# One decoder layer on one core: the compressed tokens' first layer over 129 columns, two moved steps, and a two-operation scaling on GpSimd

## The chip, the core and the metric

The kernel runs on one core of a Trainium2 chip. The metric is the device time of one execution in microseconds. Every time below comes from runs of the kernel before the change: three timed executions, and one more that was profiled.

## What is computed

One layer of a hybrid decoder for 512 tokens of width 1024, in float32. The normalised input feeds two mixers side by side: an RWKV-7 time mixing (16 heads of 64, written as chunks of 64 tokens, with a triangular inversion in each) and a sparse attention (16 heads in 4 groups, with a compressed, a selected and a sliding-window branch). Their outputs are gated, merged and projected; a gated MLP with a short convolution follows. The change touches three places of this. The compressed branch makes its keys and values so:

```
n_cmp = (S - CMP_BLOCK) // CMP_STRIDE + 1            # 31 blocks of 32 tokens, 16 apart
cidx = np.arange(n_cmp)[:, None] * CMP_STRIDE + np.arange(CMP_BLOCK)[None, :]
def compress(t, pos, w1, w2):
    blk = kv(t)[:, :, cidx] + pos.astype(f32)
    hid = jax.nn.gelu(blk.reshape(B, G, n_cmp, CMP_BLOCK * DH) @ w1.astype(f32))
    return hid @ w2.astype(f32)
```

The RWKV side shifts each projection by a token (`z = z + (prev - z) * mu`), and the attention's two softmaxes are scaled per query, each row of probabilities by one factor.

## The kernel before

Everything is one long program for TensorE, with the other four engines around it. Projections are taken in blocks of 128 output columns (`proj_steps`, L302): eight steps of three matmuls of 512 columns each (L306 to L308), since each float32 product is made of three products of split halves. These blocks are the filler: `drive` runs them as a generator, `fill`, and after each step of it lets other generators (threads, each with a delay and a rate) take a step. So a `yield` more or less in a thread moves its instructions by some steps of the filler in TensorE's order. A scheduling layer puts each engine's instructions in an order of its own from the order in which the code issues them, unless they are pinned with `keep_in_program_order`.

Compression. `cproj` (L384) makes, for keys and then for values, a tile KC of 128 partitions with 5 x 8 x 33 numbers: four groups and, as a fifth, the position part; the sixteen offsets of a pair of tokens are spread over partitions and the second index. The unused numbers are set to zero by GpSimd (L387, L390). `compress` (L405) multiplies it with the first layer's weights w1 in 16 float32 matmuls of 5 x 31 = 155 columns that add up in one PSUM bank, hid; a `yield` after every four of them puts filler between (L414). Column 124, the position part's first, becomes the bias hb (L417), which is added to the other 124 (L421). Then come a GELU and the second layer. `compress(0)` and `compress(1)` run one after the other as a thread beside the projections of pair 0.

RWKV. The 16 heads are worked on in eight pairs p, and the pairs in two groups of GP = 4. `inputs` (L493) makes K, R and V of a pair: a projection into a PSUM bank (`pj`, two banks), ScalarE's scaled copy `shift_a` (L333), then VectorE's `shift_b` (L336), which reads the bank once more and so frees it. K's `shift_b` is put in the code at the step SK = 4 of R's projection, pinned. `prep` (L526) forms the scaled vectors, ending with AR (L570) and KB; `couple` (L581) multiplies R, transposes V on TensorE (tile pv, L140 by way of `tr`), and multiplies KB with AR (tile g, L605). When a group's four pairs are done, `invert` runs a triangular inversion on VectorE as a chain of 60 instructions (tiles TM and XP, L660 and L662), while TensorE works on gate projections (gt) and, for group 0, on pair 4's K, R and V. Then the inverse is copied and transposed to TT (L674 to L683), and `recur` starts with matmuls on it (mt, L703).

Attention. For each of eight pairs of heads p8, `score` (L1051) makes the scores of both heads by blocks of 128 queries, their exponentials p with row sums (L1097, L1099), and in `norm` multiplies each tile p by its factor from stt (L1073): branch b = 0 on VectorE, b = 1 on GpSimd, 64 tiles each, of 128 to 512 columns. `values` then transposes the tiles (pt, L140), copies them out of PSUM and multiplies them with the values (o, L1146). The compressed branch's probabilities, sc, are scaled by GpSimd too (L1049) and transposed as pct. The attention of p8 = 0 starts while the last RWKV work of group 1 is finished.

Of the kernel before, what the change touches and what calls it, by code (L numbers as in the profile page):

```python
# [10 lines left out]
F32 = mybir.dt.float32  # L11
F32R = mybir.dt.float32r
AF = mybir.ActivationFunctionType
OP = mybir.AluOpType
# [9 lines left out]
NCMP = 31  # L24
# [8 lines left out]
GP = 4  # L33
# [9 lines left out]
def hybrid_layer(ctx: ExitStack, tc: tile.TileContext, a, out, dbg=None, stop=None):  # L43
# [338 lines left out]
    KCs = []  # L382

    def cproj(kv):  # L384
        KC = cp.tile([128, 5, 8, 33], F32, tag="KC", name=f"KC{kv}", bufs=2)
        KCs.append(KC)
        po.memset(KC[:, 4], 0.0)  # L387
        pos = cp.tile([64, 32], F32, tag="pos", name=f"pos{kv}", bufs=2)
        sy.dma_start(pos, a["posk" if kv == 0 else "posv"])
        po.memset(KC[:, 0:4, :, 32:33], 0.0)  # L390
        for i in range(2):
            po.tensor_copy(KC[64 * i:64 * i + 64, 4, :, 0:2].rearrange("p r q -> p q r"),
                           pos.rearrange("p (q r two) -> p q r two", r=8, two=2)[:, :, :, i])
        for half in range(2):
            p = pj(f"kc{kv}{half}")
            yield from proj_steps((35 if kv == 0 else 37) + half, f"kc{kv}{half}", p)
            z = cp.tile([128, 2, 8, 32], F32, tag="z", name=f"zc{kv}{half}", bufs=2)
            pv = p.rearrange("p (q r two) -> p two r q", r=8, two=2)
            for i in range(2):
                sc.activation(z[:, i], pv[:, i], AF.Copy)  # L400
            for e in range(2):
                for i in range(2):
                    sc.dma_start(KC[64 * i:64 * i + 64, 2 * half + e, :, 0:32], z[e * 64:e * 64 + 64, i])

    def compress(kv):  # L405
        w1 = cp.tile([128, 16, 128], F32, tag="w1", name=f"w1{kv}", bufs=2)
        sy.dma_start(w1, a["w1k" if kv == 0 else "w1v"])
        w2 = cp.tile([128, 64], F32, tag="w2", name=f"w2{kv}", bufs=2)
        sy.dma_start(w2, a["w2k" if kv == 0 else "w2v"])
        ph = pz(f"hid{kv}")  # L410
        for l in range(16):
            te.matmul(ph[:, 0:5 * NCMP], w1[:, l, :], KCs[kv][:, :, l % 8, l // 8:l // 8 + NCMP],
                      start=l == 0, stop=l == 15)
            if l % 4 == 3:  # L414
                yield
        hb = cp.tile([128, 1], F32, tag="hb", name=f"hb{kv}", bufs=2)
        ve.tensor_copy(hb, ph[:, 4 * NCMP:4 * NCMP + 1])  # L417
        u = cp.tile([128, 4, 32], F32, tag="hu", name=f"hu{kv}", bufs=2)
        w = cp.tile([128, 4, 32], F32, tag="hv", name=f"hv{kv}", bufs=2)
        po.memset(u, 0.0)  # L420
        ve.tensor_scalar(u[:, :, 0:NCMP], ph[:, 0:4 * NCMP].rearrange("p (g n) -> p g n", n=NCMP), hb, None,  # L421
                         op0=OP.add)
        ve.tensor_tensor(w, u, u, op=OP.mult)
        ve.tensor_scalar(w, w, 0.044715, 1.0, op0=OP.mult, op1=OP.add)
        ve.tensor_tensor(w, w, u, op=OP.mult)
        sc.activation(w, w, AF.Tanh, scale=float(np.sqrt(2.0 / np.pi)))
        ve.tensor_scalar(w, w, 0.5, 0.5, op0=OP.mult, op1=OP.add)
        ve.tensor_tensor(u, u, w, op=OP.mult)
        yield
        yield  # L430
        pm = pz(f"kcm{kv}")
        if kv == 0:
            te.matmul(pm[0:64, 0:128], w2, u.rearrange("p g n -> p (g n)"), start=True, stop=True)
            k4 = pm[0:64, 0:128].rearrange("p (g n) -> p g n", n=32)
            sc.activation(kcs[0:64, :, 0], k4, AF.Copy)
            ve.tensor_tensor(kcs[0:64, :, 1], k4, kcs[0:64, :, 0].bitcast(F32), op=OP.subtract)
            sy.dma_start(kcs[64:128].bitcast(F32), kcs[0:64].bitcast(F32))
        else:
            for e in range(2):
                es = slice(e * 32, e * 32 + 32)  # L440
                for g in range(4):
                    te.matmul(pm[es, g * 64:g * 64 + 64], u[:, g, :], w2, start=True, stop=True)
            for q in (0, 64):
                sc.activation(vcc[q:q + 64], pm[0:64, 0:256].rearrange("p (g d) -> p g d", d=64), AF.Copy)
# [48 lines left out]
    def inputs(p, o):  # L493
        K = o.K = rw.tile([128, S], F32, tag="K", name=f"K{p}", bufs=2)
        pk = pj(f"k{p}")
        yield from proj_steps(4 + 3 * p, f"k{p}", pk)
        shift_a(pk, K, 8 + p)
        R = o.R = rw.tile([128, S], F32, tag="R", name=f"R{p}", bufs=1)
        pr = pj(f"r{p}")
        for i, _ in enumerate(proj_steps(3 + 3 * p, f"r{p}", pr)):  # L500
            if i == SK:
                tc.keep_in_program_order(shift_b(pk, K, 8 + p))
            yield
        shift(pr, R, p)
# [76 lines left out]
    def couple(p, o, gr, i):  # L581
# [4 lines left out]
            sc.activation(AR[:, 0, :], Q, AF.Copy)  # L586
        po.tensor_tensor(AR[:, 1, :].rearrange(c8, t=64), R.rearrange(c8, t=64), EC[:, :, 1:65], op=OP.mult)
        sc.activation(gr.Dc[:, i], EC[:, :, 64], AF.Copy)
        yield
        yield  # L590
        for q in range(2):
            pv = px(f"pv{p}{q}")
            for j in range(4):
# [457 lines left out]
    def score(p8, o):  # L1051
# [11 lines left out]
        def norm(e, qb, k):  # L1063
# [6 lines left out]
                                 op=OP.mult)  # L1070
            for b in range(2):
                i = b * 4 + k
                (po if b else ve).tensor_scalar(o.pe[e, b, k], o.pe[e, b, k], st[e][:, 3, i:i + 1], None, op0=OP.mult)  # L1073

        done = []
        for e, qb in ((0, 3), (0, 2), (1, 3), (1, 2), (0, 1), (0, 0), (1, 1), (1, 0)):
# [512 lines left out]
```

## Time and profile before

| | |
|---|---|
| median of 3 runs | 1169.26 us (1168.82 to 1169.72) |
| the profiled execution's own time | 1168.92 us |
| span of that execution, first to last instruction | 1167.1 us |
| instructions in the profile | 19728 |
| busy time of DVE, ACT, POOL | 587.8, 584.0, 580.5 us |

The engines are called PE (TensorE's matmuls), PEld (its weight loads), DVE (VectorE), ACT (ScalarE), POOL (GpSimd) and SP (SyncE, which issues most DMAs). A row of the timeline has the start from the beginning of the span in us, the length in us, the engine, the line of the kernel, the operation, `out<-in` by the program's names without their numbers, the shape, the count of instructions that were merged, and in square brackets the idle time before it with what ended it. A row of the groups has the count, the busy time in us and the mean length of one in ns, then the idle time before. A float32 matmul stands as two records (64 for hid's 32), a transpose as one; starts of TensorE's records are measured, their ends are modelled, so distances between starts are the better measure.

### The profile page before, as it was taken

The page shows a single profiled execution, that of the slowest core. Times are in us where ns is not written, and L with a number is a line of the kernel's source. Part 1 is how long each engine was busy: PE and PEld are TensorE (multiplying, and loading weights), DVE is VectorE, ACT ScalarE, POOL GpSimd, SP SyncE. Part 2 cuts the span into 40 slices and gives each one's busy share as a digit, 9 for nine tenths or more (in the row PEclk, how much of TensorE's full clock was granted, in tenths as well). Part 3 has the DMA queues.
Part 4 walks back from the last instruction along what each step waited for, and adds up shares of the span by engine and source line. Part 5 has one row for each costly group of instructions (what it writes and reads, how often), then busy time and mean ns, then how long its engine had stood idle before and what let it go on. Part 6 is the DMA issues. An engine that isn't in the chain of part 4 may idle for free.

```text
span 1167.1 us, 19728 instructions
## 1 busy us (share of the span) xinstructions
PE 1145.0 (98%) x7338; PEld 916.2 (79%) x7338; DVE 587.8 (50%) x1194; ACT 584.0 (50%) x1150; POOL 580.5 (50%) x526
## 2 busy tenths in 40 slices
PE   9999999999999999989999999999999999999997
PEld 7888878777887887656677778889888888888886
DVE  4226666534676642677798745754443343331103
ACT  5537664453666434567676654434444444443311
POOL 4335654425655443477766635511565566554440
PEclk9999999999999999999999999999999999999999
DMA  6433235321433664115552136641233333334421
GB/s 235 126 83 80 84 105 166 111 86 44 133 113 103 190 182 128 56 42 149 168 156 89 46 98 182 211 153 37 83 99 99 95 95 100 99 94 134 135 64 72
DMA packets 95507, 131.95 MB, mean 113 GB/s; under 512 B 34033, under 2 KB 36913, under 8 KB 95154
## 3 DMA queue, kind: packets, MB, share of 16 engines
q1 hardware_dynamic: 79490, 116.26, 33.3%
q10 hardware_dynamic: 15920, 14.42, 4.0%
q8 instruction: 58, 0.95, 0.3%
q14 instruction: 39, 0.32, 0.1%
HBM read 108.30 MB, written 19.14 MB: 109 GB/s over the span
## 4 chain that ended last, share of the span: by engine, by line
PE 91%; DVE 4%; ACT 2%; POOL 2%; issue 1%; DVEq 0%; POOLq 0%; ACTq 0%
PE pu L221 6%; PE pu L223 6%; PE pu L222 6%; PE dn L1321 3%; PE dn L1320 3%; PE dn L1319 3%; PE o L1146 3%; PE pt L140 3%; PE ub L1203 3%; PE gt L306 2%; PE ub L1205 2%; PE ub L1204 2%; PE gt L307 2%; PE gt L308 2%; PE v L306 2%; PE v L307 2%
## 5 line engine op out<-in xcount | busy, mean ns | idle before, releaser
L1099 ACT ACTIVATE p<-p,stt 128x384 f32<-128x384 f32 (+3 forms) x128 | 70.7, 554 | 35.1 <-DVE stt L1097 33.4
L1073 POOL TENSOR_SCALAR p<-p,stt 128x512 f32<-128x512 f32 (+1 forms) x64 | 72.9, 1149 | 30.7 <-DVE stt L1068 16.4
L1461 DVE SCALAR_TENSOR_TENSOR u<-pu,cvec,u 128x511 f32<-128x511 f32 x44 | 33.0, 749 | 101.1 <-ACT u L1460 101.1
L1097 DVE CUSTOM_DVE_ANT_0 p<-s,rh 128x384 f32<-128x384 f32 (+3 forms) x128 | 59.2, 485 | 24.6 <-PE s L1083 18.9
L140 PE MATMUL pt<-ident,p 128*128 128x128 f32 x320 | 44.7, 274 | 2.9 <-POOL p L1073 2.0
L1467 DVE TENSOR_TENSOR al<-u,ah 128x512 fp32r<-128x512 f32 x22 | 23.9, 1085 | 45.5 <-ACT ah L1466 45.5
L140 PEld LDWEIGHTS pt<-ident,p 128*128 128x128 f32 x320 | 37.9, 141 | 7.8 <-POOL p L1073 2.5
L1146 PE MATMUL o<-PT,vt 128*64 128x384 f32 (+3 forms) x256 | 43.9, 448 | 0.0
L1465 POOL TENSOR_TENSOR u<-u,u 128x512 f32<-128x512 f32 x22 | 28.4, 1290 | 27.2 <-DVE u L1462 26.3
L1090 PE MATMUL s<-kst,qs 128*128 128x512 f32 (+1 forms) x128 | 38.5, 390 | 2.6 <-DVE stt L1097 2.4
L1460 ACT ACTIVATE u<-pu,cvec 128x512 f32<-128x512 f32 x44 | 33.6, 765 | 3.0 <-PE pu L1423 3.0
L1462 DVE SCALAR_TENSOR_TENSOR u<-pu,cvec,u 128x510 f32<-128x510 f32 x44 | 33.0, 749 | 1.6
L1073 DVE TENSOR_SCALAR p<-p,stt 128x512 f32<-128x512 f32 (+1 forms) x64 | 33.2, 548 | 0.8
L1137 ACT ACTIVATE PT<-pt 128x512 f32<-128x512 f32 x48 | 27.6, 586 | 9.2 <-PE pt L140 8.8
L1146 PEld LDWEIGHTS o<-PT,vt 128*64 128x64 f32 x256 | 16.8, 136 | 19.4 <-issue 17.5
L1090 PEld LDWEIGHTS s<-kst,qs 128*128 128x128 f32 x128 | 21.4, 189 | 10.7 <-DVE stt L1097 6.2
L1367 DVE TENSOR_TENSOR p2ss<-p2ss 128x1 f32<-128x1 f32 x4 | 0.6, 161 | 52.1 <-ACT p2jl L1365 52.1
L1139 DVE COPY PT<-pt 128x512 f32<-128x512 f32 x32 | 21.6, 676 | 8.3 <-PE pt L140 8.3
L1466 ACT ACTIVATE ah<-u 128x512 fp32r<-128x512 f32 x22 | 13.9, 633 | 22.1 <-POOL u L1465 22.1
L1099 ACT ACTIVATION_READ_ACCUMULATOR p<-p,stt 128x1 f32 x128 | 24.1, 189 | 0.0
L809 ACT ACTIVATE UV<-xs 64x256 f32<-64x256 f32 x16 | 6.0, 378 | 35.0 <-PE xs L804 34.6
L662 DVE TENSOR_TENSOR XP<-XP,TM 128x30 f32<-128x30 f32 (+14 forms) x60 | 20.3, 338 | 2.0
(1758 smaller groups left out, 3939.4 us busy)
## 6 DMA issues: line engine op xcount, KB each, us to landing
gtd<-gt ACTq DMA_DIRECT2D x16, 256.0 KB, 2.8
qs<-qd SPq DMA_DIRECT2D x32, 128.0 KB, 3.3
g<-gtd SPq DMA_DIRECT2D x16, 256.0 KB, 3.0
xt<-in_x_dram SPq DMA_DIRECT2D x4, 512.0 KB, 5.2
bvd<-bv SPq DMA_DIRECT2D x8, 256.0 KB, 2.3
bvl<-bvd SPq DMA_DIRECT2D x8, 256.0 KB, 2.9
kst<-kst ACTq DMA_DIRECT2D x16, 128.0 KB, 2.3
t<-oad SPq DMA_DIRECT2D x8, 256.0 KB, 3.3
```

Source lines behind the costliest of these rows:

```text
L140: return te.transpose(o, i, ident)
L221: te.matmul(p, wh(k), mh(k), start=first and k == 0, stop=False)
L222: te.matmul(p, wh(k), ml(k), start=False, stop=False)
L223: te.matmul(p, wl(k), mh(k), start=False, stop=last and k == n - 1)
L306: te.matmul(p, wh(k), hh[:, k, :], start=k == 0, stop=False)
L307: te.matmul(p, wh(k), hl[:, k, :], start=False, stop=False)
L1073: (po if b else ve).tensor_scalar(o.pe[e, b, k], o.pe[e, b, k], st[e][:, 3, i:i + 1], None, op0=OP.mult)
L1090: m = te.matmul(s_[:, :n], qt, kt[:, x, b, :n], start=x == 0, stop=x == 1)
L1097: ve.tensor_tensor_reduce(sb, parts[b], rh[e][:, (3 - qb) * 128:], -1.0, BIG, OP.add, OP.min, st[e][:, 0, i:i + 1])
L1099: sc.activation(sb, sb, AF.Exp, scale=-1.0, bias=st[e][:, 0, i:i + 1], accum_out=st[e][:, 1, i:i + 1])
L1146: te.matmul(acc[e * 64:e * 64 + 64, j * 128:], vt[:, j, b * 256 + g * 64:b * 256 + g * 64 + 64], m[e][:, c:c + n], start=False, stop=k == ...
L1203: te.matmul(p, wh(k), sh[:, k, :], start=k == 0, stop=False)
```

## The change

In `cproj` and `compress`, KC becomes 128 partitions of 8 x 130 numbers. The position part takes the first two columns, the four groups 32 columns each behind it, and nothing is left to be set to zero. A product now reads 129 neighbouring columns; of the result, column 0 is the bias, and each group has 31 columns that are used and one that is not. The `yield` comes after every eight products, twice.

In `inputs`, pair 4's `shift_b` of K is issued right behind its `shift_a` and is no longer pinned. In `couple`, the last pair of each group yields three times in place of two ahead of pv. In `norm`, GpSimd's scaling multiplies by the factor and then by 1.0; VectorE's keeps its form. The rest of the file is as it was, with lines behind L405 moved by up to five.

```diff
-        KC = cp.tile([128, 5, 8, 33], F32, tag="KC", name=f"KC{kv}", bufs=2)
+        KC = cp.tile([128, 8, 130], F32, tag="KC", name=f"KC{kv}", bufs=2)
         KCs.append(KC)
-        po.memset(KC[:, 4], 0.0)
...
-        po.memset(KC[:, 0:4, :, 32:33], 0.0)
         for i in range(2):
-            po.tensor_copy(KC[64 * i:64 * i + 64, 4, :, 0:2].rearrange("p r q -> p q r"),
+            po.tensor_copy(KC[64 * i:64 * i + 64, :, 0:2].rearrange("p r q -> p q r"),
...
-                    sc.dma_start(KC[64 * i:64 * i + 64, 2 * half + e, :, 0:32], z[e * 64:e * 64 + 64, i])
+                    c = 2 + 32 * (2 * half + e)
+                    sc.dma_start(KC[64 * i:64 * i + 64, :, c:c + 32], z[e * 64:e * 64 + 64, i])
...
-            te.matmul(ph[:, 0:5 * NCMP], w1[:, l, :], KCs[kv][:, :, l % 8, l // 8:l // 8 + NCMP],
-                      start=l == 0, stop=l == 15)
-            if l % 4 == 3:
+            te.matmul(ph[:, 0:129], w1[:, l, :], KCs[kv][:, l % 8, l // 8:l // 8 + 129], start=l == 0, stop=l == 15)
+            if l % 8 == 7:
+                yield
                 yield
...
-        ve.tensor_copy(hb, ph[:, 4 * NCMP:4 * NCMP + 1])
+        ve.tensor_copy(hb, ph[:, 0:1])
...
-        ve.tensor_scalar(u[:, :, 0:NCMP], ph[:, 0:4 * NCMP].rearrange("p (g n) -> p g n", n=NCMP), hb, None,
+        ve.tensor_scalar(u[:, :, 0:NCMP], ph[:, 2:130].rearrange("p (g n) -> p g n", n=32)[:, :, 0:NCMP], hb, None,
...
         shift_a(pk, K, 8 + p)
+        if p == GP:
+            shift_b(pk, K, 8 + p)
...
-            if i == SK:
+            if i == SK and p != GP:
                 tc.keep_in_program_order(shift_b(pk, K, 8 + p))
...
-        yield
-        yield
+        for _ in range(3 if i == GP - 1 else 2):
+            yield
...
-                (po if b else ve).tensor_scalar(o.pe[e, b, k], o.pe[e, b, k], st[e][:, 3, i:i + 1], None, op0=OP.mult)
+                w = st[e][:, 3, i:i + 1]
+                if b:
+                    po.tensor_scalar(o.pe[e, b, k], o.pe[e, b, k], w, 1.0, op0=OP.mult, op1=OP.mult)
+                else:
+                    ve.tensor_scalar(o.pe[e, b, k], o.pe[e, b, k], w, None, op0=OP.mult)
```

How this stands in the engines' orders is seen at three places. The first is TensorE during the projection of k0, with the first layer's products for the keys (hid, from KC and the weights w); first the rows of before, then those of the changed kernel:

```order
L306 MATMUL k_642<-hh,k0h_643 128x512
L307 MATMUL k_642<-hl,k0h_643 128x512
L308 MATMUL k_642<-hh,k0l_644 128x512
L412 MATMUL hid_662<-KC_443,w_658 128x155 x4
L306 MATMUL k_642<-hh,k0h_643 128x512
L307 MATMUL k_642<-hl,k0h_643 128x512
L308 MATMUL k_642<-hh,k0l_644 128x512
L412 MATMUL hid_662<-KC_443,w_658 128x155 x4
```
```order
L308 MATMUL k_638<-hh,k0l_640 128x512
L411 MATMUL hid_658<-KC_443,w_654 128x129 x8
L306 MATMUL k_638<-hh,k0h_639 128x512
L307 MATMUL k_638<-hl,k0h_639 128x512
L308 MATMUL k_638<-hh,k0l_640 128x512
L306 MATMUL k_638<-hh,k0h_639 128x512
L307 MATMUL k_638<-hl,k0h_639 128x512
L308 MATMUL k_638<-hh,k0l_640 128x512
L411 MATMUL hid_658<-KC_443,w_654 128x129 x8
```

Eight products stand together, with two steps of the projection between two such bunches where one step stood between bunches of four.

The second is TensorE in front of the last pair of group 0: gate products (gt10), the transposes pv and the products g. Before, and then changed:

```order
L306 MATMUL gt_1690<-hh,gt10h_1697 128x512
L307 MATMUL gt_1690<-hl,gt10h_1697 128x512
L308 MATMUL gt_1690<-hh,gt10l_1698 128x512
L140 MATMUL pv_1720<-ident,V_1527 128x128 x4
L140 MATMUL pv_1726<-ident,V_1527 128x128 x4
L605 MATMUL g_1732<-AR_860,KB_1665 128x128
```
```order
L306 MATMUL gt_1686<-hh,gt10h_1693 128x512
L307 MATMUL gt_1686<-hl,gt10h_1693 128x512
L308 MATMUL gt_1686<-hh,gt10l_1694 128x512
L306 MATMUL gt_1686<-hh,gt10h_1693 128x512
L307 MATMUL gt_1686<-hl,gt10h_1693 128x512
L308 MATMUL gt_1686<-hh,gt10l_1694 128x512
L306 MATMUL gt_1686<-hh,gt10h_1693 128x512
L307 MATMUL gt_1686<-hl,gt10h_1693 128x512
L308 MATMUL gt_1686<-hh,gt10l_1694 128x512
L140 MATMUL pv_1722<-ident,V_1523 128x128 x4
L140 MATMUL pv_1728<-ident,V_1523 128x128 x4
L606 MATMUL g_1734<-AR_856,KB_1661 128x128
```

Two steps, six gate products, have come ahead of pv; the same move stands in group 1 with gt06.

The third is VectorE in the inversion of group 0 (TM and XP), where the second halves of pair 4's shifts (K, R, V) stand. The end of the inversion before:

```order
L662 TENSOR_TENSOR XP_1878<-XP_1878,TM_1850 128x4x27
L336 SCALAR_TENSOR_TENSOR R_2084<-r_2085,vec,R_2084 128x511
L660 TENSOR_TENSOR TM_1850<-XL_1849,XP_1878 128x84
L662 TENSOR_TENSOR XP_1878<-XP_1878,TM_1850 128x3x28
L660 TENSOR_TENSOR TM_1850<-XL_1849,XP_1878 128x58
L662 TENSOR_TENSOR XP_1878<-XP_1878,TM_1850 128x2x29
L660 TENSOR_TENSOR TM_1850<-XL_1849,XP_1878 128x30
L662 TENSOR_TENSOR XP_1878<-XP_1878,TM_1850 128x30
L336 SCALAR_TENSOR_TENSOR K_2042<-k_2043,vec,K_2042 128x511
L336 SCALAR_TENSOR_TENSOR V_2125<-v_2127,vec,V_2125 128x511
```

And in the changed kernel the places of K and of R, further up in the same inversion:

```order
L661 TENSOR_TENSOR TM_1846<-XL_1845,XP_1874 128x228
L336 SCALAR_TENSOR_TENSOR K_2038<-k_2039,vec,K_2038 128x511
L663 TENSOR_TENSOR XP_1874<-XP_1874,TM_1846 128x12x19
...
L663 TENSOR_TENSOR XP_1874<-XP_1874,TM_1846 128x7x24
L336 SCALAR_TENSOR_TENSOR R_2081<-r_2082,vec,R_2081 128x511
L661 TENSOR_TENSOR TM_1846<-XL_1845,XP_1874 128x150
```

K has moved from behind the inversion's last step to twelve steps before its end and stands ahead of R, which has moved up by three steps. Small moves of neighbours come with it (ScalarE's copies of pv behind a gate's, one load on SP ahead of another).

## The prediction

> **What bounds the kernel now.** I read the page's busy times and chain first, then the list of who waited for whom on TensorE, then the timeline around each wait.
>
> ```profile
> PE 1145.0 (98%) x7338; PEld 916.2 (79%) x7338; DVE 587.8 (50%) x1194; ACT 584.0 (50%) x1150; POOL 580.5 (50%) x526
> PE 91%; DVE 4%; ACT 2%; POOL 2%; issue 1%; DVEq 0%; POOLq 0%; ACTq 0%
> ```
>
> TensorE is busy for 98% of the span and makes 91% of the chain that ended last. So an edit is worth what it takes out of TensorE's own stream, or out of the few places where that stream stands still; time saved on another engine is worth nothing elsewhere. Of the waits, these four name an instruction that the change touches or moves (columns: total us, times, longest):
>
> ```profile
> PE pct L140 <- POOL sc L1049: 2.2, 1, 2.2
> PE pt L140 <- POOL p L1073: 2.0, 2, 1.3
> PE v L306 <- DVE R L336: 2.0, 1, 2.0
> PE g L605 <- DVE AR L570: 1.9, 2, 0.9
> ```
>
> Together they are 8.1 us, of 22 us that TensorE is idle in all.
>
> **Part 1: the compression's products, 155 to 129 columns.** One bunch of four in the timeline (start, length, engine), and the products as a whole:
>
> ```profile
> 56.59 0.39 PE L308 MATMUL k<-hh,k0l 128*128 128x512 f32 x1
> ...
> 56.82 1.24 PE L412 MATMUL hid<-KC,w 128*128 128x155 f32 x8
> ...
> 57.79 0.50 PE L306 MATMUL k<-hh,k0h 128*128 128x512 f32 x1
> ...
> 58.13 0.39 PE L307 MATMUL k<-hl,k0h 128*128 128x512 f32 x1
> ```
> ```profile
> L412 PEld LDWEIGHTS hid<-KC,w x64: 186/188/191, 56.6 to 73.4; 128*128 128x128 f32 x64
> L412 PE MATMUL hid<-KC,w x64: 293/298/399, 56.8 to 73.5; 128*128 128x155 f32 x64
> ```
>
> Each float32 product stands as two records, so 32 products are 64 records. From the L308 before the bunch to the second projection product behind it pass 58.13 - 56.59 = 1.54 us. Two ordinary steps of that stream are 0.23 us each (56.59 to 56.82), so the bunch costs 1.54 - 0.46 = 1.08 us, 0.135 us a record, 0.87 ns a column. Is it the columns that set this pace? The nearest row is a run of float32 transposes, each with a fresh 128x128 stationary operand and 128 columns:
>
> ```profile
> 539.02 0.87 PE pt L140 x8
> ```
> ```profile
> L140 PEld LDWEIGHTS pt<-ident,p 128*128 128x128 f32 x320 | 37.9, 141 | 7.8 <-POOL p L1073 2.5
> ```
>
> It goes at 0.87 / 8 = 0.109 us a record, 0.85 ns a column: the same rate per column. So 129 columns should take 0.111 us, and 64 x (0.135 - 0.111) = **1.5 us** go. The other bound is nothing: a weight load lasts 188 ns here and 141 ns in the transposes, and if that were the pace, 0.109 x 188 / 141 = 0.145 us would already exceed what is measured. That it exceeds it speaks for the columns, and I take 1.5. Bunches of eight in place of four save four changes between two kinds of product. The 1.08 us of a bunch are eight records at the pace inside it, so a change costs about nothing; its upper bound is the slow product behind a bunch, 58.13 - 57.79 - 0.23 = 0.11 us, four times 0.4 us. I take zero. The dropped memsets of KC run on GpSimd in the first microseconds and hide behind the loading of x; the sixteen DMAs into KC keep their number and runs of 32 numbers. On SP the copy of kcs now stands ahead of k10's load, which is wanted a whole projection later: nothing.
>
> **Part 2: K's second half of the token shift for pair 4, earlier on VectorE.**
>
> ```profile
> 207.17 0.39 PE L308 MATMUL r<-hh,r4l 128*128 128x512 f32 x1
> 209.55 0.50 PE L306 MATMUL v<-hh,v4h 128*128 128x512 f32 x1 [1.98 <-DVE R L336]
> ```
> ```profile
> 208.74 0.75 DVE L336 SCALAR_TENSOR_TENSOR R<-r,vec,R 128x511 f32<-128x511 f32 x1 [4.56 <-ACT R L333]
> ```
>
> v4 starts 0.06 us after R's shift ends, while K's shift still stands last in the inversion: v4 has r4's bank, since k4's comes free later. r4 had only just ended. With K's shift ahead of R's in VectorE's order, k4's bank is the first free one, and v4 waits for K alone. K's first half is done long before:
>
> ```profile
> 202.52 0.67 ACT L333 ACTIVATE K<-k,vd 128x512 f32<-128x512 f32 x1
> ```
> ```profile
> 197.39 0.39 DVE L660 TENSOR_TENSOR TM<-XL,XP 128x228 f32<-128x228 f32 x1
> ...
> 221.59 3.16 DVE L683 COPY TT<-XL 32x1024 f32<-32x1024 f32 x2
> ```
> ```profile
> 230.64 1.08 PE L703 MATMUL mt<-x 32*32 32x32 f32 x32
> ```
>
> VectorE then has K at 203.2 + 0.75 = 203.9, before r4 ends: the wait goes, 209.55 - 207.17 - 0.23 = 2.15 us, **2.2** with the slow first product behind it. The edit adds a wait: VectorE reaches K's new place at 197.8 and stands there for about 5 us, with the rest of the inversion, R, V and the copies to TT queued behind. Before, it stood 4.56 us at R instead, and only three of the inversion's steps came behind R where six do now (some 2 us more), so the queue as a whole ends within 2 us of where it did. Those who wait for it are mt's products, and they start 230.64 - 224.75 = 5.9 us after the last copy. That is the cover; it would have to be lost before this edit costs anything. Bounds: 0 (another wait takes the place) to 2.2.
>
> **Part 3: one step more in front of the last pair's pv.**
>
> ```profile
> 165.96 1.03 PE L140 MATMUL pv<-ident,V 128*128 128x128 f32 x8
> 167.95 2.06 PE L605 MATMUL g<-AR,KB 64*128 64x128 f32 x32 [0.95 <-DVE AR L570]
> ```
> ```profile
> 167.12 0.68 DVE L570 SCALAR_TENSOR_TENSOR AR<-Q,pb 128x512 f32<-128x512 f32 x1
> ```
> ```profile
> 370.79 2.06 PE L605 MATMUL g<-AR,KB 64*128 64x128 f32 x32 [0.95 <-DVE AR L570]
> ```
>
> pv ends at 165.96 + 8 x 0.109 = 166.83, and g waits until AR is there, 1.1 us. The order now puts six gate products (6 x 0.227 = 1.36 us) ahead of pv, so g comes at 168.2 in the old time, after AR's 167.80. Each group gets 1.1 us, **2.2** for both (0 to 2.2). What follows g on VectorE starts when it did, so the inversion slips against TensorE by the same 1.1 us, inside the 5.9 us above.
>
> **Part 4: GpSimd's scaling with two operations.** Grouped by shape:
>
> ```profile
> L1073 POOL TENSOR_SCALAR p<-p,stt 128x512 f32<-128x512 f32 x16 | 27.1, 1691 | 18.7 <-DVE stt L1068 12.1 <-ACT p L1099 6.5
> ...
> L1059 POOL TENSOR_SCALAR rh<-dist 128x512 f32<-128x512 f32 x16 | 10.1, 630 | 5.3 <-DVE stt L1097 4.0 <-PE y L760 0.5
> ...
> L1073 POOL TENSOR_SCALAR p<-p,stt 128x128 f32<-128x128 f32 x16 | 9.7, 605 | 0.0
> ```
>
> One operation costs (1691 - 605) / 384 = 2.83 ns a number. The row of rh, the same opcode and shape with two operations, takes 630 ns. No row has two operations with a factor per partition; the bounds are 630 ns (the second operation decides) and 1691 ns (the kind of factor decides), and I take 630, the row with the new form's count of operations. [...]
>
> About 40 us of GpSimd's busy time would go, worth something only where TensorE waits for it, at the start of the attention:
>
> ```profile
> 493.41 2.90 POOL L1073 TENSOR_SCALAR p<-p,stt 128x512 f32<-128x512 f32 x2 [2.31 <-ACT p L1099]
> 496.29 0.61 POOL L1049 TENSOR_TENSOR sc<-sc,sct 128x256 f32<-128x256 f32 x1
> 496.88 2.95 POOL L1073 TENSOR_SCALAR p<-p,stt 128x512 f32<-128x512 f32 x2
> ...
> 515.96 3.00 POOL L1073 TENSOR_SCALAR p<-p,stt 128x512 f32<-128x512 f32 x2 [5.01 <-DVE stt L1068]
> ```
> ```profile
> 496.37 0.44 PE L140 MATMUL pt<-ident,p 128*128 128x128 f32 x2 [0.67 <-POOL p L1073]
> ...
> 499.89 0.44 PE L140 MATMUL pt<-ident,p 128*128 128x128 f32 x2 [1.34 <-POOL p L1073]
> ...
> 521.60 0.63 PE L140 MATMUL pct<-ident,sc 128*64 128x128 f32 x4 [2.19 <-POOL sc L1049]
> ```
> ```profile
> 495.54 0.16 DVE L1047 TENSOR_TENSOR sct<-sct,gates 128x8 f32<-128x8 f32 x1
> ```
>
> The first two waits are 2.0 us. With pairs of at most 2 x 0.63 = 1.26 us both would go, but sc L1049 then waits for VectorE until 495.70 and ends at 496.3, where pct stands next: about 0.5 comes back, **1.5** stay. At 515.96 the pair shrinks from 3.00 to 1.26 us and everything up to sc L1049 moves up by **1.7**, leaving 0.5 of the 2.19. Third, the clock, by stretches (columns: length, then busy us of PE, PEld, DVE, ACT, POOL, then the granted clock):
>
> ```profile
> 519.47:522.89 3.42, 1.29 (x12) 1.29 (x13) 2.55 (x8) 1.80 (x6) 2.17 (x3) 1.00 0.00 0
> 522.89:526.30 3.41, 3.41 (x9) 1.37 (x7) 1.50 (x6) 1.98 (x6) 3.33 (x4) 0.50 0.22 36
> ```
>
> Behind the longest wait TensorE runs for 3.41 us at half clock, a loss of at most 1.7 us. With most of the wait gone it should not come. Whether it comes in the executions that are timed no row tells, so I take the middle of 0 and 1.7, **0.9**. [...] Part 4 is 1.5 + 1.7 + 0.9 = **4.1**, bounds 0 to 2.0 + 2.19 + 1.7 = 5.9.
>
> **Sum.** 1.5 + 2.2 + 2.2 + 4.1 = 10.0 us. The profiled execution took 1168.92 us (1167.1 of span and 1.8 around it), which gives 1158.9; the median of the runs lies 0.34 above it, so 1169.26 - 10.0 = **1159.2**.
>
> **Rivals.**
> - The factor per partition decides, not the count of operations: part 4 is zero and 1169.26 - 5.9 = 1163.4. For it: every one-operation row has such a factor and every two-operation row a number. Against: a factor per partition is one more number per partition, not one per element, and the slow row's cost grows with the elements. Chance 0.18.
> - The weight load holds the pace of the compression: part 1 is zero, 1169.26 - 8.5 = 1160.8. Against it stands the equal rate per column. 0.07.
> - The moved places find new waits (g for rbl or GS, v4 for another bank): parts 2 and 3 are zero, the change doesn't do there what it says, 1169.26 - 5.6 = 1163.7. The slack of 5.9 us speaks against it. 0.04.
> - Two or more of these at once: part 1 alone is left, 1167.8, not to be told from no change. A measurement of this kernel tells about 0.2%, 2.3 us, from nothing. 0.05.
> - Slower: GpSimd runs the second operation as a pass of its own, 5.66 ns a number. A pair of 512 and 384 goes from 2.9 to 5.4 us, and TensorE waits 2.5 longer at each of the three places, 7.6, and about 2 more in a second stretch of half clock: 7.6 + 2 - 5.9 = 3.7, 1173.0. It decides from 1.6 times the old cost on. The row at 630 ns speaks against it. 0.04.
>
> **How the numbers follow.** The forecast has 0.62. Its own range is 1157.1 (all 5.9 of part 4 and the 0.4 between the products) to 1161.6 (of part 4 the 1.7 alone). To leave no more than 2 in 10 out, the range must take in the first three rivals, 1163.7 at most, and a little of the 0.9 us by which the runs of before differ: 1157.1 to 1163.9. Faster: 0.62 + 0.18 + 0.07 + 0.04 = 0.91; same 0.05; slower 0.04.
>
> **What would show it.** Records of hid 0.111 us apart; no wait of v for R and none of g for AR; GpSimd's L1073 at about 630 ns for 512; pct's wait near 0.5 us; no stretch at half clock near 520. A GpSimd row still at 1.7 us makes it 1163; a new wait on VectorE's K, at mt above all, makes part 2 wrong.

## The result, and the profile after

| | before | after |
|---|---|---|
| median, range, runs | 1169.04 us (1168.27 to 1169.72, 4) | 1161.12 us (1159.99 to 1162.25, 4) |
| span of the profiled execution | 1167.1 us | 1158.2 us |
| GpSimd busy | 580.5 us | 544.4 us |

The ratio is 0.9932 with a 95% interval of 0.9915 to 0.995: too little for a bound of 2%, but 1 is outside it. The changed kernel is about 8 us faster; 10 had been forecast, and the time lies inside the range that was given. In a later comparison on another chip it was 1162.01 us (1159.9 to 1162.95, 6 runs) against 1168.72 us (12 runs), ratio 0.9941 (0.9927 to 0.9954).

The page after, busy times:

```profile
PE 1140.2 (98%) x7338; PEld 912.9 (79%) x7338; DVE 588.9 (51%) x1194; ACT 582.6 (50%) x1150; POOL 544.4 (47%) x522
```

Nothing in this row tells where the time went: TensorE is still busy for 98%. The list of waits does (engine and line that waited, releaser; total us, times, longest):

```profile
...
PE pg L882 <- DVE stt L1069: 1.3, 1, 1.3
PE q L308 <- POOL q5l L162: 0.9, 1, 0.9
PE pct L140 <- POOL sc L1050: 0.8, 1, 0.8
PE pg L882 <- DVE stt L1102: 0.7, 1, 0.7
...
PE gt L308 <- POOL gt17l L162: 0.6, 1, 0.6
PE pct L140 <- DVE stt L1069: 0.6, 1, 0.6
PE kcm L441 <- DVE hu L427: 0.4, 1, 0.4
PE gt L308 <- POOL gt02l L162: 0.3, 1, 0.3
```

Of the four waits named ahead of the change, v for R, g for AR and pt for GpSimd's p are gone; pct for sc fell from 2.2 to 0.8. But five rows are new: pg for stt L1102, gt for gt17l and for gt02l, pct for stt, and kcm for hu. Each is a place where something else is now late.

To see what each part is worth, the time of the execution is cut at products that both kernels have, and the starts of the same products are compared. All numbers are us between two starts in the traces (the first row: from the span's start):

| stretch on TensorE | touched by | before | after | difference |
|---|---|---|---|---|
| start to the first product of k0 | - | 56.14 | 54.05 | -2.09 |
| to the last L306 of v0 | part 1 | 26.06 | 24.89 | -1.17 |
| first of gt00 to first of k4 | part 3, group 0 | 41.21 | 41.27 | +0.06 |
| first of k4 to first of gt03 | part 2 | 18.64 | 16.32 | -2.32 |
| last L306 of gt15 to that of ksp0 | part 3, group 1 | 33.95 | 34.21 | +0.26 |
| first pc to the last L306 of q6 | part 4 | 91.61 | 87.97 | -3.64 |
| last L1208 of wb00 (L1203 before) to first of wb03 | part 4 | 41.36 | 40.87 | -0.49 |

The stretches left out differ by at most 0.07 us each; what follows the first wb03 took 0.5 us longer. The four parts together are -7.3 us, of 10.0 forecast; part 3 gave nothing. And 2.1 us were saved ahead of everything that the change is about. Three questions follow: why part 3 gave nothing, whether the start belongs to the change, and whether parts 1, 2 and 4 are worth what this one trace shows.

### The profile page after: what moved, and what is told of

Same layout as the page of the kernel before. It is cut to its first block, busy times and chain, and to the rows that moved or that the text cites. A ratio compares the mean times of both kernels' runs of the same rounds, so it can differ in the third digit from the quotient of the medians.

```text
span 1158.2 us, 19723 instructions
## 1 busy us (share of the span) xinstructions
PE 1140.2 (98%) x7338; PEld 912.9 (79%) x7338; DVE 588.9 (51%) x1194; ACT 582.6 (50%) x1150; POOL 544.4 (47%) x522
## 4 chain that ended last, share of the span: by engine, by line
PE 52%; DVE 1%; POOL 1%; issue 0%; ACT 0%; DVEq 0%; POOLq 0%; ACTq 0%
PE pu L223 6%; PE pu L221 6%; PE pu L222 6%; PE dn L1326 3%; PE dn L1325 3%; PE dn L1324 3%; PE o L1151 3%; PE ub L1208 3%; PE ub L1210 2%; PE ub L1209 2%; PE pt L140 2%; PE s L1095 1%; PE wo L1398 1%; PE wo L1396 1%; PE wo L1397 1%; PE s L1088 1%
## 5 line engine op out<-in xcount | busy, mean ns | idle before, releaser
L1102 DVE CUSTOM_DVE_ANT_0 p<-s,rh 128x384 f32<-128x384 f32 (+3 forms) x128 | 59.2, 484 | 23.6 <-PE s L1088 17.9
L1076 POOL TENSOR_SCALAR p<-p,stt 128x512 f32<-128x512 f32 (+1 forms) x64 | 38.7, 616 | 38.6 <-DVE stt L1069 25.3
L1470 POOL TENSOR_TENSOR u<-u,u 128x512 f32<-128x512 f32 x22 | 28.4, 1290 | 27.2 <-DVE u L1467 26.3
```

The source lines that it names most:

```text
L1076: po.tensor_scalar(o.pe[e, b, k], o.pe[e, b, k], w, 1.0, op0=OP.mult, op1=OP.mult)
L1102: ve.tensor_tensor_reduce(sb, parts[b], rh[e][:, (3 - qb) * 128:], -1.0, BIG, OP.add, OP.min, st[e][:, 0, i:i + 1])
```

## The experiments

### Part 3: what took its place

The timeline of after in group 0 behind the place of g. A row is start, length, engine, line, operation; in brackets the idle time before, with what ended it:

```profile
181.51 0.60 ACT L477 ACTIVATE gt<-gt 128x512 f32<-128x512 f32 x1 [4.50 <-PE gt L308]
...
182.64 1.03 ACT L656 ACTIVATE XP<-XL 128x1024 f32<-128x1024 f32 x1 [0.53 <-ACT gt L477]
...
183.60 0.61 ACT L124 ACTIVATE gt02h<-gt021r 128x512 fp32r<-128x512 f32 x1
...
183.80 0.39 PE L308 MATMUL gt<-hh,gt02l 128*128 128x512 f32 x1
...
184.30 1.28 POOL L162 TENSOR_TENSOR gt02l<-gt021r,gt02h 128x512 fp32r<-128x512 f32 x1 [6.39 <-ACT gt02h L124]
...
185.63 0.50 PE L308 MATMUL gt<-hh,gt02l 128*128 128x512 f32 x1 [0.35 <-POOL gt02l L162]
...
185.97 0.40 PE L306 MATMUL gt<-hh,gt02h 128*128 128x512 f32 x1
```

And of before, the same instructions:

```profile
182.46 1.03 ACT L655 ACTIVATE XP<-XL 128x1024 f32<-128x1024 f32 x1 [1.11 <-DMA XL<-ld]
185.84 0.60 ACT L478 ACTIVATE gt<-gt 128x512 f32<-128x512 f32 x1 [2.36 <-PE gt L308]
186.34 0.62 ACT L124 ACTIVATE gt02h<-gt021r 128x512 fp32r<-128x512 f32 x1
...
187.03 1.29 POOL L162 TENSOR_TENSOR gt02l<-gt021r,gt02h 128x512 fp32r<-128x512 f32 x1 [4.80 <-ACT gt02h L124]
...
188.81 0.39 PE L308 MATMUL gt<-hh,gt02l 128*128 128x512 f32 x1
```

Before, ScalarE copied XP while it had nothing to do and then stood at the gate's tanh (L478); the split of the next gate weight, gt02h, came right behind the tanh, and its low half from GpSimd was done at 188.32, 0.5 us before TensorE wanted it. After, the copy of XP has moved behind the tanh in ScalarE's order. ScalarE stands 4.50 us at the tanh with the copy queued behind it, and the copy, 1.03 us long, stands between tanh and gt02h. The low half is done at 185.58, too late: from 183.80 to 185.97 TensorE takes 2.17 us for five steps that are 5 x 0.227 = 1.13 us elsewhere (0.227 us is the median distance between starts of gate products in after), and 1.0 is lost, about what g had waited. Two kernels test this.

**e1_two_steps**: two steps ahead of pv again, the rest as changed.

```diff
-        for _ in range(3 if i == GP - 1 else 2):
+        for _ in range(2):
             yield
```

> The changed kernel with two steps instead of three ahead of the last pair's pv (part 3 undone). Stages on TensorE, by starts of the same products: gt00 to k4 took 41.21 us before and 41.27 changed, gt15's last step to ksp0's last step 33.95 and 34.21. Theory (the third step removes g's wait for AR, 2 x 1.05, but puts ScalarE's copy XP<-XL behind a gate's tanh, so that gt02l and gt17l come late and TensorE loses it again): g waits for AR again, about 0.95 idle each, the waits for gt02l and gt17l are gone, and both stages stay within 0.3 us of the changed kernel's. Rival (the late gt02l and gt17l come from the other edits, the third step gains 2 x 1.05): both waits on GpSimd stay and each stage is 1.0 us longer, 42.3 and 35.2.

Measured: 1160.05 us. The two stretches take 41.21 and 33.94 us, as before the change (part 1's stretch is 0.36 us longer than in after, on which more below); the waits for gt02l and gt17l are gone, and the one that part 3 had removed is back:

```profile
PE g L606 <- DVE AR L571: 1.9, 2, 0.9
```

So part 3 removes its wait and pays as much for the new one, or a little more. **e2_xp_on_vector** keeps the third step and takes the copy out of ScalarE's queue:

```diff
-        sc.activation(XP.rearrange("u i c -> u c i"), LU, AF.Copy)
+        ve.tensor_copy(XP.rearrange("u i c -> u c i"), LU)
```

> The changed kernel with the copy XP<-XL on VectorE in place of ScalarE, all else kept. Theory (that copy's place in ScalarE's order holds up gt02h and gt17h): no wait for gt02l or gt17l, gt00 to k4 about 40.1 us (41.27 - 1.1), gt15 to ksp0 about 32.9 (34.21 - 1.3); together 2.4 us less of span. Rival (the loads on SP, which now stand behind three XL loads, are what is late): both waits stay, both stages within 0.2 us of 41.27 and 34.21.

Measured: 1158.29 us, the stretches 40.47 and 33.24 us. No row of TensorE's waits names g, gt02l or gt17l. The timeline of this kernel:

```profile
179.94 1.23 DVE L656 COPY XP<-XL 128x1024 f32<-128x1024 f32 x1 [5.25 <-DMA XL<-ld]
...
182.56 0.63 ACT L124 ACTIVATE gt02h<-gt021r 128x512 fp32r<-128x512 f32 x1 [0.46 <-ACT gt L477]
...
184.25 0.39 PE L307 MATMUL gt<-hl,gt02h 128*128 128x512 f32 x1
...
184.62 0.19 PEld L308 LDWEIGHTS gt<-hh,gt02l 128*128 128x128 f32 x1 [0.41 <-POOL gt02l L162]
184.62 0.50 PE L308 MATMUL gt<-hh,gt02l 128*128 128x512 f32 x1
...
184.96 0.39 PE L306 MATMUL gt<-hh,gt02h 128*128 128x512 f32 x1
```

The split of gt02 comes 1.04 us earlier than in after. Against after the gain is 0.80 + 0.97 us, where 2.4 had been expected; against before it is 0.74 + 0.71 = 1.4 us, less than the 2.2 that part 3 was to bring. That the copy's place was what cost is shown. What is still missing stands in the last rows: gt02l is late even so. The load of these weights waits for it, and two products start 0.37 and 0.34 us behind their neighbours in place of 0.23, 0.25 us in all; the list of TensorE's waits leaves this out because the modelled ends of the products cover it. Group 1 has the same with gt17l. The step from pv to g shrinks by 1.02 us, from 1.22 to 0.20; less the 0.25, that is about the 0.74 and 0.71 measured.

### Part 4: is it the second operation, and what is it worth?

In after, GpSimd's rows by shape (count, busy us, mean ns, idle before):

```profile
L1076 POOL TENSOR_SCALAR p<-p,stt 128x512 f32<-128x512 f32 x16 | 12.9, 809 | 22.8 <-DVE stt L1069 20.4 <-ACT p L1104 2.3
...
L1060 POOL TENSOR_SCALAR rh<-dist 128x512 f32<-128x512 f32 x16 | 10.1, 633 | 10.5 <-DVE stt L1102 9.5 <-PE y L761 0.5
...
L1076 POOL TENSOR_SCALAR p<-p,stt 128x128 f32<-128x128 f32 x16 | 6.0, 373 | 0.0
```

The scaling of 512 columns fell from 1691 to 809 ns, not to 630. **e3_scale_one_op** undoes the scaling alone, and **e4_rh_one_op** takes the second operation from rh, whose factor is one number for all partitions:

```diff
-                    po.tensor_scalar(o.pe[e, b, k], o.pe[e, b, k], w, 1.0, op0=OP.mult, op1=OP.mult)
+                    po.tensor_scalar(o.pe[e, b, k], o.pe[e, b, k], w, None, op0=OP.mult)
```
```diff
-            po.tensor_scalar(rh[e], dist, float(2.0 ** (-8.0 * (h + 1) / 16)), 1.0, op0=OP.mult, op1=OP.mult)
+            po.tensor_scalar(rh[e], dist, float(2.0 ** (-8.0 * (h + 1) / 16)), None, op0=OP.mult)
```

> The changed kernel with GpSimd's scaling in its old form (part 4 undone). Theory (part 4 alone makes the attention's start faster): pc's first product to q6's last step back from 87.97 to about 91.6 us, a stretch at half clock behind the long wait of pct, the scaling of 512 columns back at 1.6 to 1.7 us. Rival (the shorter stage comes from another alignment of the work after parts 1 to 3): that stage stays within 0.5 us of 87.97.

> The changed kernel with rh made by GpSimd in one operation (a factor that is a plain number) instead of two. Theory (the count of operations decides): rh's 128x512 goes from 0.63 us to about 1.5 us, as the one-operation scaling had it. Rival (a factor per partition is what was slow): rh stays at 0.63 us.

The row of the scaling in e3, and that of rh in e4:

```profile
L1076 POOL TENSOR_SCALAR p<-p,stt 128x512 f32<-128x512 f32 x16 | 27.0, 1690 | 18.9 <-DVE stt L1069 16.5 <-ACT p L1104 2.3
```
```profile
L1060 POOL TENSOR_SCALAR rh<-dist 128x512 f32<-128x512 f32 x16 | 24.4, 1524 | 8.7 <-DVE stt L1102 7.7 <-PE y L761 0.5
```

rh without its second operation goes from 633 to 1524 ns, with the kind of factor unchanged. So in these rows the count of operations decides (1690 against 809 ns for the scaling, 1524 against 633 for rh), and the rival that the factor per partition does falls. It also shows that rh's second operation, there already, had been worth much: e4 takes 1166.39 us, since TensorE waits 4.5 us for vt at the start of the attention, where GpSimd's first four rh take 6.47 us in a row (2.71 in after), and then runs 6.81 us at half clock (487.36 to 494.17 us, granted clock 0.50).

e3's stretch in the attention took 94.77 us, 3 us more than the 91.6 expected and than the 91.61 of before with the same slow scaling; the whole took 1167.48 us. Its waits on GpSimd are shorter than those of before (pt 1.3 us in all, pct 0.9); its clock is another. Stretches of e3 (from:to, length, then busy us and count of PE, PEld, DVE, ACT, POOL, granted clock, DMA share, GB/s):

```profile
489.12:492.53 3.41, 2.01 (x10) 1.18 (x10) 3.41 (x17) 3.41 (x11) 3.41 (x4) 1.00 0.01 2
492.54:502.77 10.23, 9.64 (x32) 7.89 (x31) 5.42 (x23) 7.57 (x20) 7.27 (x9) 0.50 0.14 52
513.01:516.42 3.41, 1.81 (x10) 1.24 (x10) 3.20 (x8) 2.18 (x5) 1.83 (x2) 1.00 0.17 38
516.43:519.84 3.41, 2.93 (x12) 1.39 (x12) 1.35 (x7) 3.41 (x12) 2.17 (x3) 0.50 0.00 0
```

These are 13.6 us at half clock, against 3.41 in before. To have part 4 without this, **e5_scale_alone** puts it alone into the kernel before (the same edit of `norm`, nothing else).

> The kernel before with GpSimd's two-operation scaling and nothing else (part 4 alone). Theory (parts are independent; part 4 is worth what it was in the whole): pc's first product to q6's last step from 91.61 to about 88.0 us, no stretch at half clock near 520, GpSimd's 512 columns at about 0.8 us; the stages before it as in the kernel before (26.06, 73.11, 41.21, 18.64). Rival (it needs the earlier parts' alignment): that stage stays above 90. The start of k0's first product, 56.14 in the kernel before and 53.6 to 54.3 in five profiles with the change: theory (it hangs on the phase of the clock's windows and not on the kernel) leaves any value from 53.5 to 56.5 possible; rival (the dropped memsets make it) says 56.1 again.

Measured: 1164.7 us, span 1162.9, against 1167.1 for before: 4.2 us. The stretches that part 4 touches take 87.96 and 40.90 us, 3.65 + 0.46 = 4.1 us less than before; the other parts' stretches stand as before (26.06, 41.19, 18.62, 33.94), and the first k0 product at 56.03. That is where the rival of the dropped memsets wants it; the runs below, which have dropped them too, settle it.

### Part 1: bunches of eight or of four

The list of after has kcm waiting for hu, the result of the values' GELU, which runs as a chain on VectorE and ScalarE. In the timeline of after one step of the chain is long, and GpSimd's split of a weight starts with it:

```profile
70.74 1.43 DVE L424 TENSOR_TENSOR hv<-hv,hu 128x128 f32<-128x128 f32 x1
```
```profile
70.73 1.29 POOL L162 TENSOR_TENSOR v0l<-v01r,v0h 128x512 fp32r<-128x512 f32 x1 [4.83 <-ACT v0h L124]
```
```profile
73.24 0.86 PE L441 MATMUL kcm<-w,hu 128*32 128x64 f32 x16 [0.36 <-DVE hu L427]
```

The step ends at 72.17, as v0l ends at 72.02. In before, the same step (L425) stands clear of v0l and takes a fifth of that:

```profile
75.07 0.29 DVE L425 TENSOR_TENSOR hv<-hv,hu 128x128 f32<-128x128 f32 x1
```

So bunches of eight moved the chain onto the split, 1.1 us are lost there, and 0.36 of them reach TensorE. In e1 the keys' kcm (L432) waits 0.3 us for hu as well, and part 1's stretch took 25.25 us. **e6_fours** keeps the 129 columns in bunches of four:

```diff
-            if l % 8 == 7:
-                yield
+            if l % 4 == 3:
                 yield
```

> The changed kernel with the 129-column products in bunches of four, one step apart, as before. Theory (a change between kinds of product costs about nothing, and the bunches of eight only leave the values' GELU too little time, since kcm waits 0.5 us): k0 to v0's last step goes from 24.89 to about 24.4 us, with no wait of kcm. Rival (eight at a time saves four changes of 0.11 us or more): the stage is 25.3 us or longer, wait or no wait.

Measured: 1161.8 us; part 1's stretch takes 24.65 us, against 24.89 with eights and 26.06 before, and no row names kcm. The long step of the chain is at 0.29 us again. So the wait went and 0.24 us came back, less than the 0.36 of the wait alone. The rest, 0.12 us, would be what fours themselves cost; e8 gives a second value for it.

### Part 2 undone

**e7_shift_back** takes pair 4's shift back to its old place:

```diff
-        if p == GP:
-            shift_b(pk, K, 8 + p)
...
-            if i == SK and p != GP:
+            if i == SK:
```

> The changed kernel with pair 4's second half of K's shift where it was (part 2 undone). Theory (v4's wait was for r4's bank alone): v4 waits about 2.0 us for R again and k4 to gt03 goes from 16.32 to about 18.6 us, nothing else changes. Rival (part 2 only moved a wait that would have gone with the other parts): the stage stays below 17.

Measured: 1163.86 us; the wait of v for R is back with its 2.0 us, but the stretch takes 20.20 us, not 18.64. The timeline of e7 behind the wait:

```profile
206.20 0.50 PE L306 MATMUL v<-hh,v4h 128*128 128x512 f32 x1 [1.98 <-DVE R L336]
206.54 0.45 PE L307 MATMUL v<-hl,v4h 128*128 128x512 f32 x1
206.79 0.63 PE L308 MATMUL v<-hh,v4l 128*128 128x512 f32 x1
207.21 0.63 PE L306 MATMUL v<-hh,v4h 128*128 128x512 f32 x1
```

Starts go from 0.25 to 0.42 us apart: the granted clock is 0.50, for 3.4 us. The stretches by clock, of e7 and then of before, same columns as above:

```profile
203.34:206.75 3.41, 1.43 (x6) 0.86 (x5) 1.29 (x4) 1.21 (x2) 1.29 (x2) 1.00 0.34 121
206.76:210.16 3.40, 3.40 (x9) 2.63 (x8) 2.79 (x10) 0.00 (x0) 0.00 (x0) 0.50 0.26 82
```
```profile
205.45:208.86 3.41, 2.11 (x10) 1.42 (x8) 0.12 (x1) 1.21 (x2) 1.99 (x2) 1.00 0.61 196
208.86:212.28 3.42, 2.73 (x12) 2.24 (x13) 2.51 (x8) 0.65 (x1) 0.53 (x1) 1.00 0.38 105
512.64:516.05 3.41, 2.07 (x10) 1.42 (x9) 2.04 (x8) 1.03 (x4) 0.09 (x1) 1.00 0.25 70
...
519.47:522.88 3.41, 1.28 (x12) 1.28 (x13) 2.55 (x8) 1.80 (x6) 2.16 (x3) 1.00 0.00 0
522.88:526.30 3.42, 3.42 (x9) 1.38 (x7) 1.50 (x6) 1.98 (x6) 3.33 (x4) 0.50 0.22 36
```

The changes of the clock within one trace lie a whole number of times 3.413 us apart: in before, full speed is on record from 14.30 us, the clock falls to half at 522.89 and again at 1164.59, 149 and 337 times that later; in after, full speed is on record from 5.49 us, and the clock falls at 8.90 and at 1155.78, one and 337 times that later. So the changes lie on a grid in both, and the windows of before above lie on it. The same wait of 2 us falls into one window in e7 (1.43 us busy, then half clock) and is split over two in before (2.11 and 2.73 us busy, full clock). So it seems to be the place of the wait on the grid that decides, an inference from these two traces; and the grid lies otherwise in each of them: carried back to the start of the span, its first edge lies 0.65 us behind it in before and 2.08 in after. No run moved one against the other by itself.

### A mended kernel, and the start

**e8_both_mended** has the changed kernel's four parts, e2's copy on VectorE and a third `yield` ahead of kcm's products:

```diff
         yield
+        yield
         pm = pz(f"kcm{kv}")
...
-        sc.activation(XP.rearrange("u i c -> u c i"), LU, AF.Copy)
+        ve.tensor_copy(XP.rearrange("u i c -> u c i"), LU)
```

> The changed kernel with XP<-XL copied by VectorE and one step more between the GELU and kcm. Theory: no wait of kcm, gt02l or gt17l; k0 to v0 about 24.4 us, gt00 to k4 40.5, gt15 to ksp0 33.2; about 2.3 us less than the changed kernel, 1158.8 against its median of 1161.1. Rival (the waits move on once more): less than 1 us gained.

Measured: 1159.46 us (1157.51 to 1159.81, 5 runs), ratio to before 0.9921 (0.9907 to 0.9936). Stretches 24.47, 40.45 and 33.19 us; the waits for hu, gt02l and gt17l are gone. Part 1's stretch is 0.18 us shorter than with fours: if it is the four changes between two kinds of product that eights save, each is worth 0.045 us; the third step differs too, so this stays an estimate. (Here too the step of the values' GELU takes 0.29 us, clear of v0l.) The first k0 product, though, stands at 55.78, where e2 with the same code up to there has it at 54.05.

The last three runs have the changed kernel as it is, the mended one and e7's kernel side by side on one chip.

> The changed kernel itself, unaltered, so that the next two can be compared with it on one chip. Theory that the start depends on where the clock's first step falls: the first k0 product comes anywhere from 53.5 to 56.2 us, and the times spread over 2.5 us, around 1161. Rival, that the change itself shortens the start by 2 us: the first k0 product stands near 54.0 and the times stay within 1 us. Stages, either way: 24.9, 41.25 and 34.2 us, and 87.97 in the attention's.

> Third step before kcm's products, and VectorE's copy of XP, as before. Theory: 0.4 + 0.8 + 1.0 = 2.2 us below the changed kernel's median of this same call, about 1158.9, whatever the start does; the stages at 24.5, 40.5 and 33.2 us. Rival: the two copies cost VectorE something later, and the median lies within 0.8 us of the changed kernel's.

> Part 2 undone again. Theory that the clock's window decides what the wait for R costs: the wait stays at 2.0 us, the stage takes 18.6 us in executions where the wait is split between two windows and 20.2 where it falls into one, so the times lie 2.3 to 3.9 us above the changed kernel's and spread wider than its. Rival, that undoing part 2 in the changed kernel always costs the half clock: 20.2 us again, and a median 3.9 us above the changed kernel's.

| | median (us) | range, runs | first k0 product | k4 to gt03 |
|---|---|---|---|---|
| e9_after_again | 1162.01 | 1159.9 to 1162.95, 6 | 56.12 | 16.32 |
| e10_mended_again | 1159.59 | 1157.66 to 1159.69, 5 | 56.05 | 16.32 |
| e11_shift_back_again | 1164.42 | 1162.69 to 1166.07, 7 | 56.04 | 20.20 |

The mended kernel's stretches are 24.47, 40.49 and 33.20 us, as expected. Those of e9 are too, but for the attention's: 88.86 us in place of 87.97. There one more s waits for stt L1102 (2.7 us in five waits, 2.2 in four in after). The code is the same, so this is a difference of the execution, the one of 1162.95 us; why that s waited was not followed.

The unaltered changed kernel started its k0 product at 54.05 us in one execution and at 56.12 in another. The first, then e9:

```profile
1.59 3.78 PE L116 MATMUL warm<-zero 128*128 128x512 f32 x4 [1.59 <-DVE zero L111]
5.30 2.06 PE L119 MATMUL gb<-g1r 1*128 1x512 f32 x4
7.44 1.42 PE L140 MATMUL n1p<-ident,n1xn 128*128 128x128 f32 x8
```
```profile
1.59 3.78 PE L116 MATMUL warm<-zero 128*128 128x512 f32 x4 [1.59 <-DVE zero L111]
5.30 3.78 PE L119 MATMUL gb<-g1r 1*128 1x512 f32 x4
9.01 2.02 PE L140 MATMUL n1p<-ident,n1xn 128*128 128x128 f32 x8
```

The same four products take 2.06 or 3.78 us. In the first execution full speed is on record from 5.49 us; in before, whose four products take 3.78 us too and whose first k0 product stands at 56.14, from 14.30. So the 2.1 us at the start are not the change's. e9's times stand in two groups, 1159.9 and 1160.1, and 1162.0 to 1163.0; e10's too, 1157.7 twice and 1159.6 to 1159.7. That these are the two kinds of start is likely, as in both kernels the groups are 2 us apart, but the changed kernel has one trace of each kind, and the mended kernel has only traces of the late one (e8 and e10).

The mended kernel's slowest run is below the changed kernel's fastest; the medians differ by 2.4 us, where 2.2 were expected, and the two groups by 2.3 and 2.4. Undoing part 2 costs 2.4 us in the median, nearer to the 2.3 of the wait alone than to the 3.9 with half a clock behind it. Both traces of that kernel show the half clock (0.50 behind windows busy for 1.43 us in e7 and 1.41 in e11), e5's and before's with the same wait don't (behind it products start 0.23 to 0.24 us apart). If it always came, no run should lie below 1159.9 + 3.9 = 1163.8 us, and 1162.69 does; how often it comes was not settled.

## Why the prediction was right, and where it was wrong

**What bounds the kernel**: right. Some 36 us of GpSimd's busy time went, and the time fell only where TensorE had waited.

**Part 1, 1.5 us**: the size of the product term holds. In after a bunch of eight runs from the L308 at 54.50 to the L307 at 56.75, 2.25 - 0.46 = 1.79 us for sixteen records, 0.112 us each (0.111 forecast), 0.87 ns a column as with 155. With fours and no new wait (e6) the stretch is 26.06 - 24.65 = 1.4 us shorter, with the third step (e8) 1.6. What was missed is the new wait of kcm for hu, which left 1.2: the prediction weighed the changes between products, but not that bunches of eight shift the GELU behind them against GpSimd's splits.

**Part 2, 2.2 us**: right, 2.3 in the trace, 2.4 in the medians of e9 and e11, in which starts and clocks are mixed. No wait of mt came up. The new wait on VectorE came, but shorter than forecast: it stands 2.03 us at K's new place (about 5 forecast) and 0.46 us at R. The cover held: mt's first product still starts 225.09 - 219.21 = 5.9 us after the last copy to TT.

**Part 3, 2.2 us**: wrong. The step that failed is "Each group gets 1.1 us". g did lose its wait; but ScalarE's copy of XP was moved behind the gate's tanh and delayed gt02's and gt17's splits by about as much. "The inversion slips against TensorE by the same 1.1 us" fails with it: the inversion starts behind that copy, 31.9 us after the first product of gt00 in after (183.91 - 152.01) and 28.4 in before (183.72 - 155.31), 3.5 us later. mt did not wait for it all the same: VectorE stood 2.5 us at K and R in place of 4.56 at R. The rival "the moved places find new waits" described this in kind, but named other waits and weighed it with the slack of VectorE's queue alone. Of ScalarE's copies the part said nothing, and that queue, one block later, is where the new wait arose.

**Part 4, 4.1 us**: the sum is right (4.1 in e5), by terms that partly miss. The shift of the same products between before and e5 grows by 1.6 at the first two waits (1.5 forecast), by 1.3 at pct (1.7: the pair there takes 1.56 us, not 1.26, since the rows are 809 and not 630 ns on the average) and by 1.3 behind it, where the half clock is gone (0.9). Then 0.2 is gained at an s and 0.7 given back at pg, which now waits for stt L1102, and 0.4 is gained later, at 613 us of before, where s had waited. The last three were not foreseen and nearly cancel; that the sum fits to 0.1 us is in part luck. The rows at 1690 and 1524 ns with one operation (e3, e4), against 809 and 633 with two (after), bear out the choice by the count of operations, though not its 630 for the scaling. The stretch at half clock in before stood behind a window in which TensorE was busy for 1.28 of 3.41 us; in e7 and e3 such stretches stood behind windows of 1.43, 1.81 and 2.01 us.

**The range and the size**: forecast 10.0 us, the four parts 7.3 in the traces, the medians 7.9 and 6.7 on two chips. Nearly all of the difference to the traces is part 3. The spans of the two profiled executions differ by 8.9 us; 2.1 of it is the start, which is luck of the execution.

## What to carry to other kernels

Where a step of filler more is put ahead of a waiting product, look at every engine that takes part in the filler, one block further on: what stood in a gap there (here ScalarE's copy of XP, 1.03 us) may now stand behind an instruction that waits (here 4.50 us). Try a second operation, even if it only multiplies by 1.0, on a float32 `tensor_scalar` of GpSimd that multiplies: on 128x512 it took the scaling from 1690 to 809 ns (e3 against after), and rh takes 633 ns with it and 1524 without (after against e4). And compare kernels by starts of the same products, stretch by stretch: the whole moved by 2.1 us with the start (54.05 and 56.12 us to k0), and one wait of 2 us with half a clock behind it cost 1.56 us more than without (20.20 against 18.64 us, e7 and before), about as much as each part was worth.

## What the hardware showed that was not expected

In GpSimd's scaling, a float32 `tensor_scalar`, one operation takes 2.83 ns a number ((1690 - 604)/384 in e3), two take (809 - 373)/384 = 1.14 on the average in after. The scaling takes 809 ns and rh 633, with the same shape and count of operations. In after, all sixteen scalings of that shape overlap one of VectorE's own scalings (p<-p,stt) and take 694 to 933 ns; of the sixteen rh, the two that overlap one take 711 and 724 ns, the fourteen others 620 to 623. In before, five rh overlap one and take 609 to 705 ns, the eleven others 619 to 623. So a longer time goes with an overlap in after, but an overlap alone does not make one. No run tested this.

A product of VectorE and a split of GpSimd that started together took longer, now one and now the other. The product L424 of the values' GELU (hv<-hv,hu, 128x128) takes 1.43 us in after, where v0l starts 0.012 us ahead of it (70.729 and 70.741 us), and 1.43 us in e1, e2, e3, e7, e9 and e11 too. It takes 0.29 us in before, e5, e6, e8 and e10; in before, e6 and e8, v0l ends 0.45 to 1.22 us ahead of it. The keys' product, in after, starts 0.001 us ahead of the split r0l; it takes 0.29 us, and r0l 1.45 in place of the 1.29 in before, where the product starts 0.49 us behind r0l's end. Who starts first may decide; these two pairs do not show it.

Six windows of 3.41 us at full clock were followed by one to three windows at half clock. TensorE was busy in them for 0.00 us (e4), 1.28 (before), 1.41 (e11), 1.43 (e7), 1.81 and 2.01 (both e3). In before and in after, between the start of k0 and the down projection's end, no window with 2.07 us or more was followed by it; the least busy of these had 2.07 us in before and 2.09 in after. At the start of after, a window of 3.20 us busy was followed by one at half clock, so the busy time alone does not decide there. Busy time here has modelled ends, so the bound between 2.01 and 2.07 holds for this measure in these traces and is not a number of the chip.
